# Dense gates, staging tiles and the last gathers of a PEER block: one-hots in one operation, token-innermost products, no separate end stage

## The chip, the cores and the metric

The kernel runs on one core of one Trainium2 chip. The metric is the device time of one execution in microseconds (us): a median of 3 runs of the kernel before is shown, and its profile comes from one further execution. A core has five engines, each with its own queue of instructions that it takes strictly in order: TensorE (PE in the rows, its weight loads PEld), VectorE (DVE), ScalarE (ACT), GpSimd (POOL) and SyncE (SP). Here SP issues the ordinary transfers and POOL the gathers of table rows.

## What is computed

The input is 1024 tokens of 1024 numbers. First a mixer: a normalisation, a projection to 1536 columns, a pooling half and a gated half, an output projection and a residual, giving `h`. Then the PEER layer, which most of this case is about:

```
q = (xb @ wq).reshape(T, 8, 2, 128)
s = einsum('thpd,phkd->thpk', q, keys)            # 8 heads, 2 lists of 128 keys
s_top, i_top = top_k(s, 16)                       # 16 of each list
best_s, best_pos = top_k(all 16*16 sums, 16)      # the best 16 pairs of each head
idx = 128 * key_of_list_0 + key_of_list_1         # one of 16384 experts
gate = softmax(best_s)
act = gelu(einsum('td,thkd->thk', xb, u_tab[idx]))
out = einsum('thk,thkd->td', gate * act, v_tab[idx])
```

So each token uses 128 experts (8 heads of 16), each a row of 4 KB in `peer_u` and one in `peer_v`. At the end the residual is added and the rows are normalised once more.

## The kernel before, in words

The 1024 tokens are 8 blocks of 128. The kernel treats them in two ways.

**Sparse blocks** 0, 1, 6 and 7 gather the rows they need. `sparse_u` (U0, U1, U6, U7) gathers 128 times 128 rows of `peer_u`; each gather of 512 KB is followed by one multiply-and-sum on DVE (`junk`, line 501). `sparse_v` (V0, V1, V6, V7) gathers rows of `peer_v` four gathers at a time, a quad; 8 matmuls into `po` (line 531) use up one quad, with a weight tile `wz` that ACT has written (line 520). There are two `wz` tiles, so that the write for quad j waits until the matmuls of quad j-2 are done. The gathered rows lie in a ring of 7 buffers (`rowt`), in the dense stage with 4 more (`rowv`), and after it in 16 (`rowe`).

**Dense blocks** 2 to 5 (512 tokens) multiply with all 16384 experts. For this `gates_dense` first builds the gate of every token and expert. For 4 tokens at a time it makes one-hot matrices of the two key lists (`oh`): on DVE one operation for all of list 0 (line 567), one for list 1 of two tokens (line 569) and one for each of the other two tokens with the gate multiplied in (line 581); ACT multiplies the gate into the first two (line 579). One matmul for each token (line 582) gives a 128 by 128 product in PSUM; two ACT operations (line 585) copy it into two half staging tiles `gs`, turned so that tokens are innermost. When 32 tokens are done, two transfers write the halves to the DRAM tensor `G` (line 589). This happens 128 times for 4 tokens, here called 128 groups, in four blocks of 32. Between the blocks DVE chooses the experts of the next block (`pick`).

Then `scale` multiplies the transposed activations `sd` by the row norms and splits them into two parts, `xdh` and `xdl`. `dense` runs over 128 chunks of 128 experts: load `raw_u` and `raw_v`, split each, 24 matmuls of 512 columns up (`mu<-xdh,...`), gelu, times the gates `gc` read back from `G` (line 645), split into `wh` and `wl`, and 24 matmuls down for each chunk, which are issued for three chunks together (`GROUP`), with the results added to `hD` on DVE (line 623).

What sets the order: the program is woven by generators (`weave`, `sparse`, `anchors`), and a scheduler orders the instructions of each engine from it. The plan `LATE` holds 704 gathers. While the dense chunks are written, 672 of them are called for; the last 32 (`AFTER`) are in a stage of their own behind the dense one, with new row buffers `rowe` in a pool that reuses the space of the dense stage.

```
        while done * NK < (c + 1) * (steps - AFTER):
    ...
    with tc.tile_pool(name="gae", bufs=EROWS, side="right", ...) as gae:
```

Of the kernel before, what the change touches and what calls it, by code (L numbers as in the profile page):

```python
# [47 lines left out]
GS = 3  # L48
# [5 lines left out]
ROWS, VROWS, EROWS = 7, 4, 16  # L54
# [12 lines left out]
def hybrid_block(ctx: ExitStack, tc: tile.TileContext, t: dict, out: bass.AP):  # L67
# [235 lines left out]
    def residual(fc, fr, chunks, most):  # L303
# [6 lines left out]
        for q in range(4):  # L310
            cols = slice(q * WC, (q + 1) * WC)
            for ch, p in zip(chunks, project(fr, "w_out", q * WC, [ch.a for ch in chunks], True)):
                nc.vector.tensor_add(ch.h[:, :, cols], ch.h[:, :, cols], p)

                def quarter(ch=ch, q=q, cols=cols):
                    hg = tmp(fr, 2 * WC).rearrange("p (k e) -> p k e", e=WC)
                    nc.vector.tensor_mul(hg, ch.h[:, :, cols], g2row[:, None, cols].to_broadcast([P, NB, WC]))
                    if not d0 <= ch.t0 // P < d0 + DBLK:
                        nc.sync.dma_start(gS[ch.t0:ch.t0 + N, cols].rearrange("(k p) e -> p k e", p=P), hg)
# [85 lines left out]
    def pick_heads(tk, top, tix, n, keys, gate_kh):  # L405
# [46 lines left out]
        for i in range(2):  # L452
            eq = tk.tile([P, TK, TK, PH], BF16, name="eq", tag="eq", bufs=1)[:, :, :, :n]
# [59 lines left out]
    def sparse_v(b):  # L513
# [4 lines left out]
        for j in range(32):  # L518
            z = wz[j % 2]
# [34 lines left out]
    def gates_dense(gp, b):  # L554
# [4 lines left out]
        for part in range(P // GT):  # L559
            kb = (b - d0) * (P // GT) + part  # L560
            gs = [gp.tile([P, NK // 2, GT], F32, name="gs", bufs=GS) for _ in range(2)]
            for t0 in range(0, GT, TB):

                oh = gp.tile([P, 2 * TB, NK], F32, name="oh", bufs=OH)
                tok = part * GT + t0
                half = TB // 2
                nc.vector.tensor_tensor(oh[:, 0:TB, :], iota_k[:, None, :].to_broadcast([P, TB, NK]),
                                        iT[:, 0, tok:tok + TB, None].to_broadcast([P, TB, NK]), op=ALU.is_equal)
                nc.vector.tensor_tensor(oh[:, TB:TB + half, :], iota_k[:, None, :].to_broadcast([P, half, NK]),
                                        iT[:, 1, tok:tok + half, None].to_broadcast([P, half, NK]), op=ALU.is_equal)  # L570
# [16 lines left out]
            for i, g in enumerate(gs):  # L587
                n = NK // GI // 2
                nc.sync.dma_start(G[i * n:(i + 1) * n, kb].rearrange("a i b t -> i a (b t)"),
                                  g.rearrange("i (a b) t -> i a (b t)", b=GI))  # L590

    def scale(tk, xdh, xdl):

        both = tk.tile([P, 2, ND], F32, name="both", tag="eq", bufs=1)
        r2B, x = both[:, 0, :], both[:, 1, :]
# [8 lines left out]
    def dense(de, xdh, xdl):
# [3 lines left out]
        with tc.tile_pool(name="da", bufs=2, side="right", reuse_waits="tile") as da:  # L608
# [17 lines left out]
            for c in range(NK):  # L626
# [240 lines left out]
```

## Time and profile before

| | us |
|---|---|
| median of 3 runs | 2702.26 (2700.18 to 2703.74) |
| the profiled execution, its own time | 2707.89 |
| its span in the trace | 2705.8 |
| PE busy | 2438.1, 90% of the span |
| DVE busy | 1896.4, 70% |
| POOL busy | 1198.3, 44% |
| ACT busy | 774.3, 29% |

The span is the time between the first and the last instruction of the trace. A busy share is an average over stages with different limits: in the mixer and the dense stage PE is the busy one, in the gates DVE, PE and the transfers share the work. Line numbers are those of the kernel before; in the changed kernel they are some lines lower.

### The profile page before, as it was taken

The numbers are of one execution on the slowest core, as the hardware profiler recorded it, in microseconds if no ns is written. First come the engines' busy times: TensorE is split into PE (matmuls) and PEld (weight loads), VectorE is DVE, ScalarE is ACT, GpSimd is POOL, SyncE is SP. The second block draws the span as 40 slices with busy tenths as digits, with TensorE's granted clock in tenths as the row PEclk, the third lists the DMA queues.
The fourth block names the chain that finished last, engine by engine and source line by source line (L and its number), as shares of the span: only waits on it lengthen the run. The fifth ranks groups of instructions, "written<-read, shape, count | busy, mean of one in ns | idle before, by whom it ended". The sixth has DMA issues, their size and how long they took to land.

```text
span 2705.8 us, 34765 instructions
## 1 busy us (share of the span) xinstructions
PE 2438.1 (90%) x11968; PEld 1862.7 (69%) x11968; DVE 1896.4 (70%) x4643; ACT 774.3 (29%) x1424; POOL 1198.3 (44%) x1098
## 2 busy tenths in 40 slices
PE   7997899888866467999999999999999999999993
PEld 6886788767645144777777777777777777766770
DVE  2389979987797977986776767666676766433451
ACT  3220011245635252222222222322222222222220
POOL 0034753143443544655555555465455555344004
PEclk9998999999978689999999999999999999999996
DMA  7677998599988799999999999899999999889317
GB/s 250 210 245 230 384 344 284 168 313 315 333 286 296 255 307 348 361 356 324 365 354 342 341 339 364 328 361 375 327 342 359 349 348 331 324 329 359 119 39 287
DMA packets 345392, 831.49 MB, mean 307 GB/s; under 512 B 25216, under 2 KB 158848, under 8 KB 345216
## 3 DMA queue, kind: packets, MB, share of 16 engines
q0 software_dynamic: 147456, 536.94, 54.0%
q1 hardware_dynamic: 197760, 292.33, 31.4%
q8 instruction: 95, 1.56, 0.2%
q14 instruction: 81, 0.66, 0.1%
HBM read 785.13 MB, written 44.04 MB: 306 GB/s over the span
## 4 chain that ended last, share of the span: by engine, by line
PE 67%; DVE 15%; DMA 9%; issue 5%; ACT 2%; POOL 1%; SPq 0%; POOLq 0%; ACTq 0%; DVEq 0%
PE mm L176 8%; PE mm L139 8%; PE mm L140 8%; PE mu L141 8%; PE mm L141 8%; PE mu L139 8%; PE mu L140 8%; PE po L531 8%; DVE junk L501 3%; DMA G<-gs 2%; DMA rowt<-peer_v,idxT 2%; DVE rest L372 1%; PE mm L582 1%; DMA w<-w_out 1%; PE mu L582 1%
## 5 line engine op out<-in xcount | busy, mean ns | idle before, releaser
L480 POOL DMA_INDIRECT rowt<-peer_v,idxT x432 | 500.5, 1159 | 709.0 <-PE po L531 501.6
L480 POOL DMA_INDIRECT rowv<-peer_u,idx x288 | 353.6, 1228 | 176.4 <-DVE junk L501 105.7
L480 POOL DMA_INDIRECT rowt<-peer_u,idx x224 | 261.4, 1167 | 346.5 <-DVE top L370 166.4
L139 PE MATMUL mm<-vh,wh 128*128 128x512 f32 x1024 | 400.8, 395 | 14.4 <-ACT wh L131 8.4
L141 PE MATMUL mu<-xdh,ul 128*128 128x512 f32 x1024 | 403.0, 394 | 6.6 <-DVE ul L132 6.6
L139 PE MATMUL mu<-xdh,uh 128*128 128x512 f32 x1024 | 401.2, 393 | 6.2 <-ACT xdh L131 3.7
L140 PE MATMUL mu<-xdl,uh 128*128 128x512 f32 x1024 | 401.8, 392 | 1.2 <-DVE xdl L132 0.7
L140 PE MATMUL mm<-vl,wh 128*128 128x512 f32 x1024 | 401.0, 392 | 0.1
L501 DVE SCALAR_TENSOR_TENSOR junk<-rowv,h 128x1024 bf16<-128x1024 f32 x288 | 352.0, 1222 | 44.2 <-DMA rowv<-peer_u,idx 41.2
L141 PE MATMUL mm<-vh,wl 128*128 128x512 f32 x1024 | 376.9, 392 | 0.0
L623 DVE TENSOR_TENSOR hD<-hD,mm 128x512 f32<-128x512 f32 x344 | 225.8, 682 | 184.4 <-PE mm L141 183.5
L501 DVE SCALAR_TENSOR_TENSOR junk<-rowt,h 128x1024 bf16<-128x1024 f32 x224 | 271.9, 1214 | 19.6 <-DMA rowt<-peer_u,idx 18.2
L531 PE MATMUL po<-rowt,wz 128*32 128x512 f32 x1728 | 237.8, 650 | 38.0 <-DMA rowt<-peer_v,idxT 38.0
L139 PEld LDWEIGHTS mm<-vh,wh 128*128 128x128 f32 x1024 | 193.0, 189 | 75.1 <-issue 14.2
L141 PEld LDWEIGHTS mu<-xdh,ul 128*128 128x128 f32 x1024 | 192.6, 188 | 65.8 <-DVE ul L132 9.4
L139 PEld LDWEIGHTS mu<-xdh,uh 128*128 128x128 f32 x1024 | 192.1, 188 | 58.7 <-issue 9.2
L140 PEld LDWEIGHTS mu<-xdl,uh 128*128 128x128 f32 x1024 | 192.8, 188 | 53.8 <-issue 9.2
L141 PEld LDWEIGHTS mm<-vh,wl 128*128 128x128 f32 x1024 | 192.6, 189 | 50.1 <-issue 9.2
L140 PEld LDWEIGHTS mm<-vl,wh 128*128 128x128 f32 x1024 | 193.2, 189 | 42.4 <-issue 2.5
L644 ACT ACTIVATE a<-mu 128x512 f32<-128x512 f32 x128 | 76.0, 594 | 491.2 <-PE mu L141 490.0
L132 DVE SCALAR_TENSOR_TENSOR ul<-raw_u,uh 128x1024 fp32r<-128x1024 f32 x128 | 156.2, 1220 | 78.3 <-ACT uh L131 78.3
L131 ACT ACTIVATE vh<-raw_v 128x1024 fp32r<-128x1024 f32 x128 | 131.0, 1052 | 235.8 <-PE mm L141 216.9
(167 smaller groups left out, 3374.3 us busy)
## 6 DMA issues: line engine op xcount, KB each, us to landing
raw_u<-uT SPq DMA_DIRECT2D x128, 512.0 KB, 6.9
raw_v<-peer_v SPq DMA_DIRECT2D x128, 512.0 KB, 7.2
G<-gs SPq DMA_DIRECT2D x32, 1024.0 KB, 14.8
w<-wq SPq DMA_DIRECT2D x48, 512.0 KB, 6.6
w<-w_in SPq DMA_DIRECT2D x36, 512.0 KB, 4.8
w<-w_out SPq DMA_DIRECT2D x24, 512.0 KB, 6.6
h<-x SPq DMA_DIRECT2D x16, 512.0 KB, 7.7
rowt<-peer_v,idxT POOLq DMA_INDIRECT x432
```

The costliest lines, as they stand in the source:

```text
L131: nc.scalar.activation(hi, src, AF.Copy)
L132: nc.vector.scalar_tensor_tensor(lo, src, 1.0, f32(hi), op0=ALU.mult, op1=ALU.subtract)
L139: nc.tensor.matmul(dst, lh, rh, start=first and c == 0, stop=False)
L140: nc.tensor.matmul(dst, lh, rl, start=False, stop=False)
L141: nc.tensor.matmul(dst, ll, rh, start=False, stop=last and c == n - 1)
L176: mm = nc.tensor.matmul(dst[:, i, :], lhs, rhs, start=c == 0, stop=c == NDC - 1)
L480: ins = nc.gpsimd.indirect_dma_start(out=rowt, out_offset=None, in_=t[table], in_offset=bass.IndirectOffsetOnAxis(ap=ids, axis=0))
L501: nc.vector.scalar_tensor_tensor(junk, r, 1.0, h, op0=ALU.mult, op1=ALU.mult, accum_out=act[:, j:j + 1])
L531: mm = nc.tensor.matmul(po[g * 32:(g + 1) * 32, q * HALF:(q + 1) * HALF], z[:, g, 31 - j:63 - j], r[:, q * HALF:(q + 1) * HALF], start=j = ...
L582: mm = nc.tensor.matmul(p[:, i, :], oh[:, i, :], c, start=True, stop=True)
L623: nc.vector.tensor_add(hq, hq, p)
L644: nc.scalar.activation(a, p, AF.Gelu_apprx_tanh)
```

## The change

Ten edits, as they stand in the diff:

- Gates: one DVE operation makes the one-hots of both lists for 4 tokens; ACT multiplies the gate into all four tokens; the products are written to PSUM with tokens innermost, as `p[:, :, i]`, so each matmul writes every fourth word; one ACT operation copies 4 tokens into a whole staging tile; one transfer of 2 MB writes 32 tokens to `G`. Two whole tiles take the place of three pairs' worth of halves (`GS = 3`, 2 at a time).
- Four `wz` tiles, not two.
- The activations of the middle tokens lie in a mixer tile, are also written to a DRAM tensor `sS`, and are read back by `scale` (4 loads). `scale` is called ahead of the remaining gates and no longer behind the last pick.
- `wh` and `wl` have 3 buffers, not 4.
- All 704 gathers of `LATE` are called for by chunk 125. The stage behind `dense`, its pool and `AFTER` are gone.

```
-    for i in range(2):
+    for i in range(4):
         z = const.tile([P, 4, 63], F32, name=f"wz{i}")
...
+                    if D0 <= ch.t0 < D0 + ND:
+                        nc.sync.dma_start(sS[2 * q:2 * q + 2, :, ch.t0 - D0:ch.t0 - D0 + N]
+                                          .rearrange("c p s -> p c s"), sq)
...
-            z = wz[j % 2]
+            z = wz[j % len(wz)]
...
-            gs = [gp.tile([P, NK // 2, GT], F32, name="gs", bufs=GS) for _ in range(2)]
+            gs = gp.tile([P, NK, GT], F32, name="gs", bufs=2)
...
-                nc.vector.tensor_tensor(oh[:, 0:TB, :], iota_k[:, None, :].to_broadcast([P, TB, NK]),
-                                        iT[:, 0, tok:tok + TB, None].to_broadcast([P, TB, NK]), op=ALU.is_equal)
-                nc.vector.tensor_tensor(oh[:, TB:TB + half, :], iota_k[:, None, :].to_broadcast([P, half, NK]),
-                                        iT[:, 1, tok:tok + half, None].to_broadcast([P, half, NK]), op=ALU.is_equal)
+                nc.vector.tensor_tensor(oh, iota_k[:, None, None, :].to_broadcast([P, 2, TB, NK]),
+                                        iT[:, 0:2, tok:tok + TB, None].to_broadcast([P, 2, TB, NK]), op=ALU.is_equal)
...
-                    p = ps.tile([P, TB, NK], F32, name="mm")
+                    p = ps.tile([P, NK, TB], F32, name="mm")
...
-                    if i < half:
-                        nc.scalar.activation(c, c, AF.Copy, scale=iT[:, 2, at])
-                    else:
-                        nc.vector.tensor_scalar(c, iota_k, iT[:, 1, at], iT[:, 2, at], op0=ALU.is_equal, op1=ALU.mult)
-                    mm = nc.tensor.matmul(p[:, i, :], oh[:, i, :], c, start=True, stop=True)
+                    c = oh[:, 1, i, :]
+                    nc.scalar.activation(c, c, AF.Copy, scale=iT[:, 2, tok + i:tok + i + 1])
+                    mm = nc.tensor.matmul(p[:, :, i], oh[:, 0, i, :], c, start=True, stop=True)
...
-                for g, cols in zip(gs, (slice(0, NK // 2), slice(NK // 2, NK))):
-                    nc.scalar.activation(g[:, :, t0:t0 + TB].rearrange("p k i -> p i k"), p[:, :, cols], AF.Copy)
+                nc.scalar.activation(gs[:, :, t0:t0 + TB], p, AF.Copy)
...
+        for c in range(0, NDC, 2):
+            x = de.tile([P, 2, ND], F32, name="raw_x", tag="raw", bufs=3)
+            nc.sync.dma_start(x, sS[c:c + 2].rearrange("c p s -> p c s"))
+            nc.vector.tensor_mul(x, x, r2B[:, None, :].to_broadcast([P, 2, ND]))
+            split(xdh[:, c:c + 2, :], xdl[:, c:c + 2, :], x)
...
-                wh = da.tile([P, ND], F32R, name="wh", bufs=GROUP + 1)
-                wl = da.tile([P, ND], F32R, name="wl", bufs=GROUP + 1)
+                wh = da.tile([P, ND], F32R, name="wh", bufs=GROUP)
+                wl = da.tile([P, ND], F32R, name="wl", bufs=GROUP)
...
+    scale(de, xdh, xdl)
     for _ in gates:
         pass
     for b in (6, 7):
         for _ in pick(tk, b):
             pass
         turn(b)
-    scale(tk, xdh, xdl)
...
-        while done * NK < (c + 1) * (steps - AFTER):
+        while done * (NK - GROUP) < min(c + 1, NK - GROUP) * steps:
             next(gathered, None)
             done += 1
-
-    with tc.tile_pool(name="gae", bufs=EROWS, side="right", reuse_waits="tile") as gae:
-        beside[:] = [(gae, "rowe", EROWS)]
-        homes["U"] = homes["V"] = beside[:]
-        for _ in gathered:
-            pass
```

The scheduler moves instructions on every engine. Three places matter below. The first is ACT's queue in the last block of gates, before (`oh` is the multiplication by the gate, `gs` the copy of products, `wz` the weight tile for a quad):

```order
L579 ACTIVATE oh<-oh,iT 128x128 x3
L520 ACTIVATE wz_87<-wT 128x4
L585 ACTIVATE gs<-mm 128x4x64
L585 ACTIVATE gs<-mu 128x4x64
L579 ACTIVATE oh<-oh,iT 128x128 x2
L585 ACTIVATE gs<-mm 128x4x64 x2
L585 ACTIVATE gs<-mu 128x4x64
```

and the same block with the change:

```order
L580 ACTIVATE gs<-mu 128x128x4
L577 ACTIVATE oh<-oh,iT 128x128 x8
L523 ACTIVATE wz_89<-wT 128x4
L580 ACTIVATE gs<-mm 128x128x4
L577 ACTIVATE oh<-oh,iT 128x128 x4
L580 ACTIVATE gs<-mu 128x128x4
```

The `wz` writes stand between gate work in both; with four tiles in turn each waits for a quad two further back, and a group has four multiplications and one copy in place of two and two.

The second is DVE's queue where the gates end and the dense stage begins, before (`both` and `xdl` are `scale`; `idxT` is the last turned list):

```order
L402 CAST idx<-key_6262 128x128
L468 CAST idxT<-mm 128x128
L601 TENSOR_TENSOR both<-sd,both 128x512
L132 SCALAR_TENSOR_TENSOR xdl<-both,xdh 128x512
L601 TENSOR_TENSOR both<-sd,both 128x512
L542 TENSOR_TENSOR h<-h,po 128x1024
L132 SCALAR_TENSOR_TENSOR xdl<-both,xdh 128x512
```

and with the change (`ul` and `vl` are splits of loaded chunks, `a` the product with the gates):

```order
L405 CAST idx<-key_6015 128x128
L471 CAST idxT<-mm 128x128
L504 SCALAR_TENSOR_TENSOR junk,act<-rowt,h 128x1024 x2
L131 SCALAR_TENSOR_TENSOR ul<-raw_u,uh 128x1024
L131 SCALAR_TENSOR_TENSOR vl<-raw_v,vh 128x1024 x2
L504 SCALAR_TENSOR_TENSOR junk,act<-rowt,h 128x1024 x2
L131 SCALAR_TENSOR_TENSOR vl<-raw_v,vh 128x1024
L639 TENSOR_TENSOR a<-a,gc 128x512 x2
```

The 8 pairs of `scale` are gone from here; as 4 pairs of double size they stand among the operations of the last pick. On PE three chunks of up-matmuls (72) stand ahead of the first down-matmul with the change, two (48) before; 29 quads of V0 stand ahead of the last gate matmuls with the change, all 32 before, and `wt` of U1 (the end of U1) moves from chunk 11.75 to 16.25.

The third is the end of POOL's queue, before:

```order
L480 DMA rowt<-peer_v,idxT 128x1024 x4
L480 DMA rowv<-peer_v,idxT 128x1024 x4
L480 DMA rowt<-peer_v,idxT 128x1024
L480 DMA rowe<-peer_v,idxT 128x1024 x32
L863 UNCONDITIONAL_BRANCH
```

and with the change:

```order
L483 DMA rowt<-peer_v,idxT 128x1024 x4
L483 DMA rowv<-peer_v,idxT 128x1024 x4
L483 DMA rowt<-peer_v,idxT 128x1024
L850 UNCONDITIONAL_BRANCH
L850 ISA
```

No gather uses `rowe` any more; on PE the last 8 quads, which stood behind the last dense matmul, now stand in pairs up to chunk 123.9. V7's 16 pairs stand between chunks 106.2 and 123.9 (1.18 chunks apart), before 12 pairs between 103.3 and 116.7 (1.22 apart).

## Rows read from the trace of the kernel before

**Rows 1.** The page's busy times: us, share of the span, instructions.

```profile
PE 2438.1 (90%) x11968; PEld 1862.7 (69%) x11968; DVE 1896.4 (70%) x4643; ACT 774.3 (29%) x1424; POOL 1198.3 (44%) x1098
```

**Rows 2.** The span cut at the ends of stages: from and to, length, busy us (and instructions) of each engine, granted share of TensorE's clock, busy share of the transfer engines, GB/s.

```profile
559.20:655.00 95.80, 82.03 (x506) 63.59 (x503) 67.37 (x181) 57.31 (x147) 36.43 (x35) 0.95 0.95 325
655.00:745.00 90.00, 77.67 (x468) 61.34 (x468) 74.78 (x257) 54.28 (x139) 36.32 (x32) 0.91 0.93 315
745.00:787.00 42.00, 20.66 (x105) 12.32 (x105) 38.15 (x166) 9.73 (x24) 17.36 (x18) 0.68 0.83 290
787.00:860.00 73.00, 59.47 (x363) 46.77 (x361) 58.44 (x195) 44.48 (x113) 31.58 (x28) 0.88 0.81 269
860.00:925.00 65.00, 21.23 (x99) 8.24 (x99) 59.97 (x291) 11.95 (x31) 28.45 (x25) 0.60 0.83 295
925.00:1013.60 88.60, 58.31 (x354) 40.31 (x358) 70.24 (x170) 47.18 (x126) 46.02 (x36) 0.81 0.87 293
1013.60:1048.00 34.40, 24.79 (x89) 13.60 (x81) 27.19 (x50) 12.63 (x20) 19.21 (x15) 0.95 1.02 366
1048.00:1200.00 152.00, 134.40 (x567) 105.82 (x568) 137.31 (x210) 38.01 (x50) 86.67 (x66) 0.97 0.96 351
1200.00:2300.00 1100.00, 1098.88 (x5261) 822.66 (x5260) 767.34 (x1106) 297.93 (x421) 601.44 (x503) 1.00 0.94 347
2300.00:2510.00 210.00, 210.00 (x1103) 148.25 (x1105) 87.14 (x119) 53.29 (x86) 89.06 (x87) 1.00 0.88 329
2510.00:2635.80 125.80, 125.70 (x564) 102.36 (x559) 62.26 (x93) 36.81 (x50) 0.00 (x0) 1.00 0.25 80
2635.80:2705.80 70.00, 23.40 (x129) 5.59 (x128) 12.84 (x51) 3.56 (x10) 29.96 (x32) 0.71 0.71 278
```

**Rows 3.** The end in order of time: start, duration, engine, line, operation, in brackets the idle time before and what ended it.

```profile
2495.57 0.94 POOL L480 DMA_INDIRECT rowt<-peer_v,idxT  x1 [0.31 <-PE mu L141]
2646.23 0.94 POOL L480 DMA_INDIRECT rowe<-peer_v,idxT  x1 [149.72 <-DMA out<-hD]
...
2635.43 0.39 PE L141 MATMUL mm<-vh,wl 128*128 128x512 f32 x1
...
2643.08 1.28 DVE L551 SCALAR_TENSOR_TENSOR hD<-hD,r,fgrow 128x1024 f32<-128x1024 f32 x1
...
2701.03 1.28 DVE L551 SCALAR_TENSOR_TENSOR h<-h,r,fgrow 128x1024 f32<-128x1024 f32 x1
```

**Rows 4.** PE in the middle of the dense stage, same columns: a quad and matmuls around it.

```profile
1816.23 1.94 PE L531 MATMUL po<-rowt,wz 128*32 128x512 f32 x16
1818.11 0.74 PE L141 MATMUL mm<-vh,wl 128*128 128x512 f32 x2
1818.69 0.40 PE L140 MATMUL mu<-xdl,uh 128*128 128x512 f32 x1
1818.92 0.40 PE L141 MATMUL mu<-xdh,ul 128*128 128x512 f32 x1
```

**Rows 5.** Gate work. First DVE at the first group in order of time, then groups of instructions over the whole span: line, engine, operation, out<-in, count, busy us, mean ns of one, idle time before.

```profile
559.19 0.69 DVE L567 TENSOR_TENSOR oh<-iota_k,iT 128x512 f32<-128x512 f32 x1
...
560.65 0.68 DVE L567 TENSOR_TENSOR oh<-iota_k,iT 128x512 f32<-128x512 f32 x1
...
L501 DVE SCALAR_TENSOR_TENSOR junk<-rowv,h 128x1024 bf16<-128x1024 f32 x288 | 352.0, 1222 | 44.2 <-DMA rowv<-peer_u,idx 41.2
...
L579 ACT ACTIVATE oh<-oh,iT 128x128 f32<-128x128 f32 x256 | 85.3, 387 | 36.0 <-DVE oh L569 35.5
...
L585 ACT ACTIVATE gs<-mm 128x256 f32<-128x256 f32 x128 | 71.8, 633 | 66.4 <-PE mm L582 33.4 <-DMA G<-gs 32.4
...
L644 ACT ACTIVATE a<-mu 128x512 f32<-128x512 f32 x128 | 76.0, 594 | 491.2 <-PE mu L141 490.0 <-DVE wl L132 1.2
...
L220 ACT ACTIVATE vn<-mm,r1s 128x256 f32<-128x256 f32 x16 | 6.7, 470 | 15.5 <-PE mm L176 15.5
...
L582 PE MATMUL mm<-oh 128*128 128x128 f32 x512 | 86.8, 316 | 36.4 <-ACT oh L579 36.4
```

**Rows 6.** Waits between 540 and 1030 us: engine, line waited for, us in total, times, longest.

```profile
ACT wz L520 <- PE po L531: 61.9, 20, 18.4
...
PE mm L582 <- ACT oh L579: 36.4, 24, 5.4
...
ACT gs L585 <- DMA G<-gs: 32.4, 9, 8.2
DVE oh L567 <- PE mm L582: 32.2, 14, 7.3
```

**Rows 7.** Two quads of V0 on PE, in order of time; four more stand between them.

```profile
865.49 3.67 PE L531 MATMUL po<-rowt,wz 128*32 128x512 f32 x16 [4.07 <-DMA rowt<-peer_v,idxT]
...
937.69 3.52 PE L531 MATMUL po<-rowt,wz 128*32 128x512 f32 x16 [2.91 <-DMA rowt<-peer_v,idxT]
```

**Rows 8.** Where the gates end: the last copies of products, the load of gates in the chain that ended last, and the first down-matmul.

```profile
1012.57 1.06 ACT L585 ACTIVATE gs<-mu 128x256 f32<-128x256 f32 x2 [1.02 <-PE mu L582]
...
1028.64 17.84 DMA gc<-G
...
1047.98 0.50 PE L139 MATMUL mm<-vh,wh 128*128 128x512 f32 x1 [0.98 <-ACT wh L131]
```

More of the change, by code (lines that the diff above doesn't have):

```diff
@@ L47 @@
 OH = 3
-GS = 3
 BEHIND = (3, 2)
 TURN = 6
-ROWS, VROWS, EROWS = 7, 4, 16
+ROWS, VROWS = 7, 4
 QUAD = 4
@@ L108, in hybrid_block @@
     gS = dram.tile([S, D], F32, name="gS")
+    sS = dram.tile([NDC, P, ND], F32, name="sS")
     G = dram.tile([NK // GI, ND // GT, P, GI, GT], F32, name="G")
@@ L317, in quarter @@
                     nc.vector.tensor_mul(hg, ch.h[:, :, cols], g2row[:, None, cols].to_broadcast([P, NB, WC]))
-                    if not d0 <= ch.t0 // P < d0 + DBLK:
+                    if not D0 <= ch.t0 < D0 + ND:
                         nc.sync.dma_start(gS[ch.t0:ch.t0 + N, cols].rearrange("(k p) e -> p k e", p=P), hg)
@@ L452, in pick_heads @@
         for i in range(2):
-            eq = tk.tile([P, TK, TK, PH], BF16, name="eq", tag="eq", bufs=1)[:, :, :, :n]
+            eq = tk.tile([P, TK, TK, PH], BF16, name="eq", bufs=1)[:, :, :, :n]
             nc.vector.tensor_tensor(eq, iota_a[:, :, None, :n].to_broadcast([P, TK, TK, n]),
@@ L560, in gates_dense @@
             kb = (b - d0) * (P // GT) + part
-            gs = [gp.tile([P, NK // 2, GT], F32, name="gs", bufs=GS) for _ in range(2)]
+            gs = gp.tile([P, NK, GT], F32, name="gs", bufs=2)
             for t0 in range(0, GT, TB):
-                oh = gp.tile([P, 2 * TB, NK], F32, name="oh", bufs=OH)
+                oh = gp.tile([P, 2, TB, NK], F32, name="oh", bufs=OH)
                 tok = part * GT + t0
-                half = TB // 2
-                nc.vector.tensor_tensor(oh[:, 0:TB, :], iota_k[:, None, :].to_broadcast([P, TB, NK]),
-                                        iT[:, 0, tok:tok + TB, None].to_broadcast([P, TB, NK]), op=ALU.is_equal)
-                nc.vector.tensor_tensor(oh[:, TB:TB + half, :], iota_k[:, None, :].to_broadcast([P, half, NK]),
-                                        iT[:, 1, tok:tok + half, None].to_broadcast([P, half, NK]), op=ALU.is_equal)
+                nc.vector.tensor_tensor(oh, iota_k[:, None, None, :].to_broadcast([P, 2, TB, NK]),
+                                        iT[:, 0:2, tok:tok + TB, None].to_broadcast([P, 2, TB, NK]), op=ALU.is_equal)
@@ L586, in gates_dense @@
                 yield
[L587 to L595, printed above, removed]
+            nc.sync.dma_start(G[:, kb].rearrange("a i b t -> i a (b t)"),
+                              gs.rearrange("i (a b) t -> i a (b t)", b=GI))
@@ L596, in scale @@
+    def scale(de, xdh, xdl):
+        r2B = de.tile([P, ND], F32, name="r2B", tag="a", bufs=2)
         p = ps.tile([P, HALF], F32, name="mm")[:, :ND]
@@ L599, in scale @@
         nc.scalar.activation(r2B, p, AF.Copy)
-        for c in range(NDC):
-            nc.vector.tensor_mul(x, sd[:, c, :], r2B)
-            split(xdh[:, c, :], xdl[:, c, :], x)
+        for c in range(0, NDC, 2):
[3 more added lines that the diff above has]
+            split(xdh[:, c:c + 2, :], xdl[:, c:c + 2, :], x)
     def dense(de, xdh, xdl):
@@ L748, in hybrid_block @@
     first = group(FIRST, ma[1:])
-    middle = group(MIDDLE, [sd[:, :, i * N:(i + 1) * N] for i in range(len(MIDDLE))])
     last = group(LAST, ma[1:])
@@ L753, in hybrid_block @@
     fc = opened(fcs, name="fc", bufs=1, side="right")
+    middle = group(MIDDLE, [fc.tile([P, NDC, N], F32, name=f"s{i}") for i in range(len(MIDDLE))])
     later.append(lambda: stats(0, NB))
```

9 lines of the change are left out of this document (3 added, 6 removed).

## The prediction

> **What bounds the kernel now.** I read the busy times first. PE is busy for 90% of the span [rows 1], so time can be won only where PE is idle or does work of another kind. Then I read the stretches. From 1200 to 2510 us PE is never idle (1098.9 of 1100 and 210.0 of 210 us) at full granted clock, so the dense stage is bound by its matmuls. What is added to PE there is paid in full; what DVE, ACT, POOL or the transfers (busy share 0.94) get there costs nothing as long as that holds [rows 2]. Two places have slack. One is the end: after the last dense matmul 70.0 us pass with PE busy for 23.4 of them [rows 2]. The other is the gates, the six stretches from 559.2 to 1013.6 us, 454.4 us long. Their PE times sum to 319.4 and their DVE times to 369.0 us; the transfers are busy for 0.81 to 0.95 of them, and no engine is full throughout [rows 2]. There I read the waits. ACT stands for 61.9 us at a `wz` write until a quad's matmuls have ended, and for 32.4 us at a copy into `gs` until a transfer to `G` has landed; behind it PE waits 36.4 us for scaled one-hots, and behind PE DVE waits 32.2 us for a one-hot buffer [rows 6]. So ACT's queue, which is far from full, holds up the two engines that are nearly full.
>
> **End stage.** POOL issues its last gather of the dense stage at 2495.57 us, then waits 149.72 us until `out<-hD` has read the space that `rowe` reuses, and starts the last 32 gathers at 2646.23 [rows 3]. Without that stage the dense end remains: the last matmul starts at 2635.43, the last `hD` operation ends at 2644.36, 8.6 us after the stretch's end at 2635.8. Then the output must be stored, for which I take what passes after the last operation now (2702.31 to the span's end at 2705.8, 3.5 us). So 12.1 of 70.0 us stay: **-57.9 us** [rows 2, 3].
>
> The 8 quads move to PE in the dense stage. A quad occupies PE there from 1816.23 to 1818.11, 1.88 us [rows 4]; with a little for the change of weights, 1.9 each: **+15.2 us**, on the path. Their gathers need room. From 2510 to 2635.8 POOL does nothing and the transfers are at 0.25 [rows 2], while 32 gathers of 512 KB are 16.8 MB, 48 us at the 347 GB/s of the long dense stretch. The order spaces V7's pairs as far apart as before (1.18 chunks against 1.22), and PE had no idle time at that spacing [rows 2], so I expect no wait there.
>
> **Gates, DVE.** A group's one-hots step by 1.46 us (559.19 to 560.65). One operation of 1024 columns is bounded by `junk`, also two inputs and 1024 columns, 1.22 us; consecutive ones overlap by about 0.08, as the steps show, so 1.14 [rows 5]. That saves 0.32 us for each of 128 groups, 10 us for each block of 32, 41 us in all.
>
> **Gates, ACT.** A group has two scalings (0.387) and two copies (0.633) now, 2.04 us; then four scalings and one copy. The copy of 512 contiguous words costs 0.594. The copies of 256 that write single words 128 bytes apart cost 0.633 where contiguous ones cost 0.470, so 0.64 ns more for each word [rows 5]. The new copy writes runs of four words. I bound it by 0.594 and 0.594 + 0.33 = 0.92 and take 0.65, nearest to the contiguous row: 2.20 us for a group, 20 us more in all. ACT is busy for 225 of 454 us [rows 2]; this is hidden.
>
> **Gates, waits.** With four `wz` tiles a write waits for the quad four back, two quads or some 29 us longer ago [rows 7], so nearly all of the 61.9 us go. With two whole staging tiles a copy waits for the transfer of two tiles back, not of half a tile: the 32.4 us go too. The 36.4 and 32.2 us behind them shrink [rows 6]. What is late next: in the first two stretches PE itself (82.0 of 95.8, 77.7 of 90.0) and the transfers (0.95, 0.93), so I take half of PE's idle time, 7 and 6 us. In the picks (745 to 787 and 860 to 925) DVE is full already; nothing is won, and `scale` comes into the second with 4 pairs of 1024 columns, 8 x 1.14 = 9 us, half of which I expect to find idle places: +5. From 787 to 860 DVE falls from 58 to 48 and PE has 59, so 62 of 73 us: -11. From 925 on DVE falls from 70 to 60, PE has 2 or 3 quads less than its 58, and 4.5 quads at 14.4 us each (865.49 to 937.69 is 5 steps) need 65: 66 of 88.6 us, -22 [rows 2, 7]. Sum **-41 us**, with ends at -10 (the gathers set the pace everywhere) and -65 (all of DVE's saving and half of what is left of its 85 idle us).
>
> **Token-innermost products.** Each of 1024 matmul instructions now writes every fourth word of PSUM. No row has such a write on PE. The nearest is ACT's copy above, 0.64 ns for each word set apart, which would be 82 ns for 128 columns and 84 us in all [rows 5]; the other end is nothing. [...]
>
> **Scale.** Moved ahead, it leaves the place where the gates end. There it hid behind the gates' way through DRAM anyway: the last copies start at 1012.57, `gc<-G` is loaded from 1028.64 for 17.84 us, and the first down-matmul starts at 1047.98 [rows 8]. That wait stays, so nothing is won by the move itself. In its shade PE can do a third chunk of up-matmuls (24 at 0.23, **-5.4 us**) [rows 4] and two of the three V0 quads that have come behind the gates; the third is paid, **+1.9 us**. U1 ends 4.5 chunks later; up to 1200 us, with U1 running, PE lost 17.6 of 152 us [rows 2], and for 54 us more of it I take **+4 us** (0 to 6). The 8 stores to `sS` (256 KB) and 4 loads add 4 MB, 12 us of transfers at 347 GB/s, beside matmuls; I put 0, ends -3 and +3.
>
> **`wh` and `wl`, 3 buffers.** The first `wh` of three chunks must now wait for the last down-matmul of the three before, as `vh` already does. At worst its 0.63 us comes ahead of `vh` each time, 42 times, 27 us; the order leaves PE 4.7 us of up-matmuls or more there nearly everywhere, so I take 0.
>
> **Sum.** -57.9 + 15.2 - 41 - 5.4 + 1.9 + 4 = -83.2 us. The profiled execution took 2707.89 (span 2705.8 and 2.1 around it), 5.6 above the median; the terms are differences, so I take them from the median: 2702.3 - 83.2 = **2619 us**, with 2598 to 2640 as its own range.
>
> **Rivals.**
> *The gathers pace the gates.* V0 uses the 7 row buffers almost one quad at a time, and PE waits for rows at both quads shown [rows 7]. If 21 quads keep the 15.7 us they have on average, the stage shrinks by 10 and not 41: 2650. Against it: with ACT free the quads come as soon as rows land.
> *Strided products, mildly slow.* 84 us on PE bring its work to 319 - 8 + 84, and with some 40 us of idle time the stage is 435: -19, time 2641. [...]
> *Strided products, very slow: slower than before.* The products occupy PE for about 170 us (twice 86.8). From 1.9 times that on, 146 us more, the stage is 497 us and eats the other gains (42.2 us). At three times it would be 691 us, the time 2897. For it: nothing hides PE there. Against it: PE would have to be held by writes alone.
> *The split waits.* 27 us in the dense stage: 2646.
> *The end stage does not vanish.* If the last quads wait for rows, up to 43 us come back: 2662. Against it is POOL's idle time from 2497 on.
>
> **How the numbers follow.** Forecast 0.66, gathers 0.11, mildly slow products 0.09, split 0.05, end 0.03, very slow products 0.06. A difference under 0.2% (5.4 us) can't be told from none: only a product price just near 1.9 times gives that, 0.02, of the last case, which leaves slower 0.05; all else is faster, 0.93. From 2590 to 2652 the range holds the forecast and most of the cases up to 2650.
>
> **What would show it.** Right: the last quads at full PE before the last down-matmul and some 12 us after it; ACT without `wz` waits in the gates; products at the same mean duration; the last copy of products near 970 us. Wrong: matmuls of the products lengthened; quads still 15 us apart or more with PE waiting for rows; PE idle between groups of three chunks.

## The result and the profile of the changed kernel

The changed kernel takes 2639.98 us (median of 4 runs, 2637.79 to 2640.96), the kernel before 2701.22 in the same runs: a ratio of 0.9772 (95% interval 0.9755 to 0.9789), 61.2 us less. The forecast was 2619 us, 83 us less; its range of 2590 to 2652 holds the time, its own range of 2598 to 2640 only with its upper end. The profiled executions, 2707.89 and 2640.66 us, are 67.2 us apart. The busy times of the changed kernel, to be read against [rows 1]:

```profile
PE 2421.6 (92%) x11968; PEld 1855.0 (70%) x11968; DVE 1855.1 (70%) x4251; ACT 788.4 (30%) x1548; POOL 1209.1 (46%) x1100
```

Its stretches follow, with the columns of [rows 2]. The cuts are the events of the changed kernel: first and second block of gates together, the pick for the third, the third block, the pick for the fourth, the fourth block up to the last copy of products, the seam up to the first down-matmul, then the dense stage and the end:

```profile
560.20:724.00 163.80, 147.36 (x923) 117.96 (x927) 115.29 (x224) 119.39 (x343) 76.21 (x57) 0.96 0.98 329
724.00:758.20 34.20, 16.98 (x99) 10.56 (x91) 33.89 (x163) 6.09 (x15) 14.10 (x13) 0.80 0.95 335
758.20:839.00 80.80, 68.81 (x421) 53.47 (x422) 61.74 (x142) 58.08 (x170) 48.43 (x36) 0.92 0.90 290
839.00:907.40 68.40, 16.56 (x75) 4.34 (x73) 59.03 (x261) 9.53 (x19) 25.26 (x22) 0.63 0.83 288
907.40:988.60 81.20, 59.65 (x362) 44.30 (x366) 65.67 (x90) 56.10 (x164) 46.08 (x34) 0.85 0.89 300
988.60:1019.30 30.70, 15.63 (x85) 10.49 (x77) 8.36 (x11) 7.20 (x9) 12.09 (x11) 0.80 0.97 328
1019.30:1200.00 180.70, 172.55 (x745) 137.40 (x749) 160.72 (x253) 48.05 (x66) 96.64 (x77) 0.98 0.96 354
1200.00:2300.00 1100.00, 1093.27 (x5224) 813.48 (x5217) 766.15 (x1104) 291.45 (x416) 595.97 (x507) 1.00 0.94 347
2510.00:2626.10 116.10, 115.75 (x582) 83.54 (x580) 53.37 (x91) 29.10 (x44) 27.57 (x29) 1.00 0.56 204
2626.10:2638.40 12.30, 0.00 (x0) 0.00 (x0) 8.45 (x37) 1.15 (x2) 0.00 (x0) 0.60 0.43 171
```

The gates of the kernel before, cut again at the same five events:

```profile
559.20:741.40 182.20, 156.10 (x950) 121.61 (x948) 138.56 (x422) 110.51 (x284) 69.76 (x64) 0.93 0.94 319
741.40:774.80 33.40, 15.24 (x88) 9.75 (x87) 33.15 (x159) 5.52 (x11) 13.11 (x13) 0.78 0.87 308
774.80:865.30 90.50, 69.72 (x408) 53.69 (x408) 72.34 (x242) 52.65 (x135) 39.97 (x36) 0.82 0.82 275
865.30:919.90 54.60, 17.92 (x83) 5.43 (x83) 49.78 (x253) 6.19 (x15) 23.50 (x21) 0.59 0.81 286
919.90:1013.60 93.70, 60.38 (x362) 42.09 (x366) 75.12 (x185) 50.07 (x134) 49.82 (x40) 0.79 0.87 293
```

From the two executions, with the forecast beside them:

| piece | before | after | difference | forecast |
|---|---|---|---|---|
| start to the first one-hot | 559.2 | 560.2 | +1.0 | 0 |
| gates: blocks 1 and 2 | 182.2 | 163.8 | -18.4 | |
| pick for block 3 | 33.4 | 34.2 | +0.8 | |
| block 3 | 90.5 | 80.8 | -9.7 | |
| pick for block 4 | 54.6 | 68.4 | +13.8 | |
| block 4 | 93.7 | 81.2 | -12.5 | |
| gates together | 454.4 | 428.4 | **-26.0** | **-41** |
| last copy to first down-matmul | 34.4 | 30.7 | -3.7 | 0 |
| first to last down-matmul | 1587.8 | 1606.8 | +19.0 | +15.7 |
| end | 70.0 | 12.3 | **-57.7** | **-57.9** |
| span | 2705.8 | 2638.4 | -67.4 | -83.2 |

The gates hold nearly all of the miss inside the profile, 15.0 of 15.8 us; what the other pieces missed cancels but for 0.8 us. The rest of the 21 us is the reference: the sum was taken off the median, and the profiled execution before was some 6 us above it.

What a group of four tokens costs now, by line, with the columns of [rows 5]: the one-hots, the scaling, the copy, the two kinds of products (L569, L577, L580 and L578 answer to L567, L579, L585 and L582):

```profile
L569 DVE TENSOR_TENSOR oh<-iota_k,iT 128x1024 f32<-128x1024 f32 x128 | 152.6, 1218 | 14.8 <-PE mm L578 11.2 <-PE mu L578 3.2
L577 ACT ACTIVATE oh<-oh,iT 128x128 f32<-128x128 f32 x512 | 159.9, 392 | 39.0 <-DVE oh L569 38.6
L580 ACT ACTIVATE gs<-mm 128x512 f32<-128x512 f32 x64 | 37.7, 589 | 16.0 <-PE mm L578 14.8
L578 PE MATMUL mm<-oh 128*128 128x128 f32 x512 | 84.1, 305 | 14.8 <-ACT oh L577 14.3
L578 PE MATMUL mu<-oh 128*128 128x128 f32 x512 | 81.3, 304 | 18.0 <-ACT oh L577 17.7
```

The one-hot of 1024 columns costs what `junk` costs, 1.22 us, as bounded by it. The products, each writing every fourth word, take 305 ns, not more than the 316 of [rows 5]. The copy of 512 words takes 589 ns where two of 633 stood. And the waits from 540 to 1030 us, as in [rows 6]:

```profile
ACT wz L523 <- PE po L534: 57.9, 13, 16.5
...
PE po L534 <- DMA rowt<-peer_v,idxT: 47.3, 13, 16.3
ACT oh L577 <- DVE oh L569: 38.6, 24, 7.6
...
PE mu L578 <- ACT oh L577: 17.7, 21, 2.2
PE mm L578 <- ACT oh L577: 14.3, 16, 4.2
...
DVE oh L569 <- PE mm L578: 11.2, 12, 3.7
```

ACT's wait for a transfer to `G` is gone, and the waits of PE for `mm` products and of DVE that stand in [rows 6] are less than half. But the wait at `wz`, which four tiles were to remove, is still 57.9 us, from 61.9.

Part of the shorter gates is work that moved: in the kernel before 28 quads of V0 and 56 row operations of U1 (`junk`) lie in the stage, with the change 26 and 54.

At the end PE works without a gap up to the last down-matmul, and the last operation follows 8 us later; these answer to [rows 3]:

```profile
2625.69 0.39 PE L140 MATMUL mm<-vh,wl 128*128 128x512 f32 x1
...
2633.35 1.28 DVE L554 SCALAR_TENSOR_TENSOR hD<-hD,r,fgrow 128x1024 f32<-128x1024 f32 x1
```

In the seam (from the last copy of products to the first down-matmul) three chunks of up-matmuls are done (72 matmuls from 982.89 to 1001.94, the first of them before the last copy), then one quad; from 1004.2 PE idles until 1019.27. The third chunk is no gain of the change: in the trace of the kernel before 72 up-matmuls stand ahead of the first down-matmul as well, not the 48 that the description of its order gives. PE's work on `mu` alone there (from and to, length, busy us and count, granted clock, transfers):

```profile
1013.60:1047.90 34.30, 23.02 (x72) 0.95 1.02 366
```

In the chain that ended last, in order of time, the last thing late there is a load of `raw_v`, issued while the last 2 MB of `G` were being written, not `gc` as in [rows 8]:

```profile
993.56 17.34 DMA raw_v<-peer_v
1010.90 1.06 ACT vh L130
...
1019.27 0.79 PE mm L138
```

### The profile page after: what moved, and what is told of

It reads as the page before. It is cut to its first block, busy times and chain, and to the rows that moved or that the text cites. A ratio compares the mean times of both kernels' runs of the same rounds, so it can differ in the third digit from the quotient of the medians.

```text
span 2638.4 us, 34312 instructions
## 1 busy us (share of the span) xinstructions
PE 2421.6 (92%) x11968; PEld 1855.0 (70%) x11968; DVE 1855.1 (70%) x4251; ACT 788.4 (30%) x1548; POOL 1209.1 (46%) x1100
## 4 chain that ended last, share of the span: by engine, by line
PE 67%; DVE 13%; DMA 11%; issue 5%; ACT 2%; POOL 1%; SPq 0%; DVEq 0%; POOLq 0%; ACTq 0%
PE mm L138 8%; PE mm L175 8%; PE mm L139 8%; PE po L534 8%; PE mu L140 8%; PE mm L140 8%; PE mu L138 8%; PE mu L139 8%; DMA rowt<-peer_u,idx 3%; DVE junk L504 3%; DMA rowt<-peer_v,idxT 2%; DMA rowv<-peer_u,idx 2%; PE mm L578 1%; PE mu L578 1%; DVE rest L375 1%
## 5 line engine op out<-in xcount | busy, mean ns | idle before, releaser
L483 POOL DMA_INDIRECT rowt<-peer_v,idxT x448 | 528.3, 1179 | 698.8 <-PE po L534 469.6
L140 PE MATMUL mm<-vh,wl 128*128 128x512 f32 x1024 | 371.0, 391 | 0.0
L534 PE MATMUL po<-rowt,wz 128*32 128x512 f32 x1792 | 243.2, 629 | 55.4 <-DMA rowt<-peer_v,idxT 47.3
L639 DVE TENSOR_TENSOR a<-a,gc 128x512 f32<-128x512 f32 x128 | 88.4, 691 | 152.9 <-ACT a L638 152.3
```

Source lines behind the costliest of these rows:

```text
L140: nc.tensor.matmul(dst, ll, rh, start=False, stop=last and c == n - 1)
L483: ins = nc.gpsimd.indirect_dma_start(out=rowt, out_offset=None, in_=t[table], in_offset=bass.IndirectOffsetOnAxis(ap=ids, axis=0))
L534: mm = nc.tensor.matmul(po[g * 32:(g + 1) * 32, q * HALF:(q + 1) * HALF], z[:, g, 31 - j:63 - j], r[:, q * HALF:(q + 1) * HALF], start=j = ...
L639: nc.vector.tensor_mul(a.rearrange("i (k t) -> i k t", t=GT), a.rearrange("i (k t) -> i k t", t=GT), gc[:, :, c % GI, :])
```

## Experiments

Each kernel was timed against the kernel before on the same chip. A ratio's interval is some 0.3% to 0.7% wide, so two variants of the changed kernel are told apart from about 10 us on; finer readings come from the stages of one profile each. For those, the gates of kernels with the gate code and plan of the changed one were 428.4, 429.3, 425.5 and 436.5 us (the last two with two weight tiles), and of the two with those of the kernel before 454.4 and 460.5: up to 7 us of scatter either way, with means 430 and 457. A stage of one profile that lies nearer to a mean than that is not told apart from it.

**The changed kernel once more**, beside some of the runs below.

> The changed kernel once more, on the chip of the next three, as their measure: 2640 us within 6, gates 428 us from the first one-hot to the last copy.

2651.1 us, ratio 0.9802 (0.9778 to 0.9826), gates 429.3 us. The time missed the expectation, the stage held it.

**1. The end stage alone.**

```
-        while done * NK < (c + 1) * (steps - AFTER):
+        while done * (NK - GROUP) < min(c + 1, NK - GROUP) * steps:
...
-    with tc.tile_pool(name="gae", bufs=EROWS, ...) as gae:
...
```

> Kernel before with one edit: all 704 gathers called for by chunk 125 and no end stage. Theory: the end falls from 70.0 to 12.3 us (-57.7), and the 8 quads cost 8 x 1.96 = 15.7 us of PE in the dense stage, so 2701.2 - 42 = 2659 us, with no wait for rows at the last quads. Rival (rows come late when 16 pairs are squeezed in): PE waits for rows in the last chunks, up to 43 us, 2665 to 2702 us.

2671.7 against 2709.1 us, ratio 0.9859 (0.9826 to 0.9892), 38 us less (29 to 47). The expected 42 lies inside the interval. Its last chunks and its end (columns of [rows 2]):

```profile
2500.00:2654.50 154.50, 154.40 (x751) 114.84 (x749) 71.99 (x114) 40.88 (x61) 29.19 (x30) 1.00 0.54 195
2654.50:2666.60 12.10, 0.02 (x1) 0.00 (x0) 8.44 (x37) 1.15 (x2) 0.00 (x0) 0.62 0.43 173
```

PE waits for no rows; the end is 12.1 us. This edit alone makes some 38 of the 61 us.

**2. Two weight tiles instead of four.**

```
-    for i in range(4):
+    for i in range(2):
         z = const.tile([P, 4, 63], F32, name=f"wz{i}")
```

> Changed kernel with two weight tiles in place of four. Theory: in the changed kernel ACT still waits 57.9 us at wz writes, so the tiles were not what freed the gates; with two the wait is some 60 to 100 us and the time 2640 to 2648 us. Rival (the forecast's view: the waits at wz held ACT, PE and DVE in the gates): 30 us or so come back, PE waits for scaled one-hots 60 us and more instead of 32, 2660 to 2670 us.

2640.1 us, ratio 0.9755 (0.9728 to 0.9782); gates 425.5. The wait at the write is 65.9 us, between the 57.9 and 66.6 of the changed kernel's two profiles, and neither the gates nor the time moves. The forecast's reading of that wait falls: what stood behind it in ACT's queue did not set the time.

```profile
ACT wz L523 <- PE po L534: 65.9, 15, 16.5
```

**3. Products contiguous, the copy turned.** The order of instructions on PE, DVE, ACT and POOL is unchanged, row for row.

```
-    p = ps.tile([P, NK, TB], F32, name="mm")
+    p = ps.tile([P, TB, NK], F32, name="mm")
...
-    mm = nc.tensor.matmul(p[:, :, i], oh[:, 0, i, :], c, start=True, stop=True)
+    mm = nc.tensor.matmul(p[:, i, :], oh[:, 0, i, :], c, start=True, stop=True)
...
-    nc.scalar.activation(gs[:, :, t0:t0 + TB], p, AF.Copy)
+    nc.scalar.activation(gs[:, :, t0:t0 + TB].rearrange("p k i -> p i k"), p, AF.Copy)
```

> Changed kernel with the products written contiguously, one token after the other, and the ACT copy turning them; the order of instructions on PE and DVE is the same. Theory (writing every fourth word costs PE nothing): the product matmuls keep their mean of 305 ns within 10 ns and their sum of 165 us; the copy goes from 589 to about 920 ns, 42 us more ACT work in the gates, most of it in ACT's idle time; total 2636 to 2655 us. Rival (the strided writes hold PE): the mean falls below 290 ns and the total to 2630 us or less.

2662.9 us, ratio 0.9830 (0.9801 to 0.9859), against 0.9755 for experiment 2 on the same chip: 23 us slower, more than either theory allowed. By line:

```profile
L578 PE MATMUL mm<-oh 128*128 128x128 f32 x512 | 88.0, 316 | 19.3 <-ACT oh L577 18.5 <-issue 0.6
L578 PE MATMUL mu<-oh 128*128 128x128 f32 x512 | 84.8, 313 | 34.3 <-ACT oh L577 31.1 <-issue 2.5 <-ACT gs L580 0.6
...
L580 ACT ACTIVATE gs<-mm 128x512 f32<-128x512 f32 x64 | 68.2, 1066 | 13.7 <-PE mm L578 12.6 <-remote 0.6
```

The contiguous products are not faster (316 and 313 ns against 305 and 304; from the start of one to the next 112 ns in the median in the kernel before, which writes them contiguously, and 112 in the changed one), so the strided ones cost PE nothing. That is measured for these FP32 matmuls of 128 columns. The copy costs 1066 ns instead of 589, 61 us in all, and that is not hidden: the gates take 445.8 us. ACT is busy for 294 of them, far from full, yet PE waits 31.1 + 18.5 us for scaled one-hots, not 17.7 + 14.3 (24.3 + 13.0 in the changed kernel's second profile), and DVE 23.5 + 11.5 for PE, not 11.2 + 3.2 (13.2 + 5.7):

```profile
PE mu L578 <- ACT oh L577: 31.1, 19, 5.8
...
PE mm L578 <- ACT oh L577: 18.5, 16, 4.2
...
DVE oh L569 <- PE mm L578: 23.5, 18, 4.4
...
DVE oh L569 <- PE mu L578: 11.5, 13, 1.8
```

**4. One-hots as before.**

```
-    nc.vector.tensor_tensor(oh, iota_k[:, None, None, :]..., iT[:, 0:2, tok:tok + TB, None]..., op=ALU.is_equal)
+    nc.vector.tensor_tensor(oh[:, 0], ..., iT[:, 0, tok:tok + TB, None]..., op=ALU.is_equal)
+    nc.vector.tensor_tensor(oh[:, 1, 0:half], ..., iT[:, 1, tok:tok + half, None]..., op=ALU.is_equal)
...
+    if i < half:
         nc.scalar.activation(c, c, AF.Copy, scale=...)
+    else:
+        nc.vector.tensor_scalar(c, iota_k, iT[:, 1, at], iT[:, 2, at], op0=ALU.is_equal, op1=ALU.mult)
```

> Changed kernel with the one-hots made as before (three kinds of DVE operation, the gate multiplied in on DVE for two of four tokens); products and the copy stay as changed. DVE gets some 41 us more in the gates, ACT 512 - 256 scalings less. Theory (DVE is the other half of what paces the gates): the gates go from 428 to 440 to 455 us, 2650 to 2667 us. Rival (the shorter ACT copies alone give the gain, as the run with contiguous products suggests): the gates stay at 428 or fall, 2630 to 2642 us.

2655.6 us, ratio 0.9815 (0.9787 to 0.9842), against 0.9802 for the changed kernel beside it: not told apart. In the gates:

```profile
568.20:1003.50 435.30, 310.91 (x1890) 226.43 (x1894) 374.60 (x1255) 182.70 (x452) 187.77 (x166) 0.84 0.93 311
```

DVE is busy for 374.6 us, 39 more than in the changed kernel, ACT for 66 less, and the stage is 435.3 us, 5 over the mean of 430, which is no more than the scatter; it also holds 27.5 quads of V0, not 26.25. The theory's 440 us or more and the rival's 428 or less are both missed, and the run does not decide between them. The DVE operation on which the forecast rested its 41 us is worth little by itself, or as much as the 256 scalings that it puts on ACT; the run can't part these two.

**5. `scale` called behind the picks again.**

```
-    scale(de, xdh, xdl)
     for _ in gates:
...
         turn(b)
+    scale(de, xdh, xdl)
```

> Changed kernel with one edit undone: scale is called behind the last picks again (it still loads from sS). Theory: the second pick shrinks from 68.4 to about 56 us, because 4 pairs of DVE work (9.7 us) and the waits for raw_x (9.4 us) leave it; behind the gates scale hides in the 30.7 us that the gates need through DRAM; the first down-matmul comes some 12 us earlier, 2628 us. Rival (gathers pace the gates): the pick shrinks but the last block of gates stretches by as much, 2640 us. Second rival (scale is needed behind the gates too): the up-matmuls wait for xdh, a chunk less fits into the shade, 2640 to 2650 us.

2635.7 us, ratio 0.9737 (0.9710 to 0.9765), not told apart from experiment 2. The stage did as expected and the total did not. The last pick takes 46.2 us and the gates 413.7, but the up-matmuls must now wait for the fourth `raw_x` behind the last gates: last copy to first down-matmul is 43.9 us, not 30.7. From the first one-hot to the first down-matmul it is 457.6 us, with one chunk of up-matmuls in it and not three; the changed kernel has 459.1.

**6. `scale` cut in two**, loads where they are, arithmetic behind the eighth-last one-hot.

```
+    scaled = scale(de, xdh, xdl)
+    next(scaled)
     for _ in gates:
...
+    with tc.issue_after(ohs[-8]):
+        for _ in scaled:
+            pass
```

> Changed kernel with scale cut in two: its four loads stay where they are (the fourth into a tile of its own), its arithmetic on DVE and ACT comes behind the 8th-last one-hot instead of into the last pick. Theory: the last pick falls from 68 to about 56 us, the last block stretches by at most 5, and since the loads are done the up-matmuls start at the last copy as now: first down-matmul some 8 to 13 us earlier, 2627 to 2632 us. Rival (gathers pace the gates, the pick's time comes back in the last block): 2638 to 2642 us.

2642.4 us, ratio 0.9786 (0.9754 to 0.9818), against 0.9802: not told apart. Block 3, the pick and block 4, first here, then in the changed kernel beside it (here the pick is cut from the start of the last one-hot before it, in the tables above from its end, which makes it 1.2 us shorter):

```profile
764.50:846.40 81.90, 68.29 (x417) 52.41 (x418) 60.43 (x140) 56.87 (x168) 47.98 (x36) 0.92 0.89 279
846.40:892.40 46.00, 13.77 (x64) 4.07 (x63) 45.96 (x248) 4.55 (x14) 16.95 (x15) 0.70 0.86 307
892.40:990.80 98.40, 65.34 (x375) 45.16 (x376) 76.87 (x102) 62.08 (x172) 59.28 (x40) 0.83 0.89 297
```

```profile
762.40:850.10 87.70, 70.26 (x409) 54.17 (x410) 60.86 (x140) 56.38 (x164) 46.60 (x36) 0.85 0.87 281
850.10:910.20 60.10, 19.17 (x88) 6.33 (x86) 60.10 (x265) 11.79 (x24) 25.55 (x22) 0.59 0.88 306
910.20:990.30 80.10, 57.86 (x362) 42.66 (x366) 65.56 (x90) 55.88 (x164) 46.06 (x34) 0.88 0.91 304
```

The pick gives back 14 us, the last block takes 18 (with 6 quads of V0 in it, not 5.25). So the place of `scale` lengthens the pick, but undoing that gains nothing. The rival said so and put it down to the gathers, which experiments 8, 9 and 11 test.

**7. An eighth of the gates stored.**

```
-    nc.sync.dma_start(G[:, kb]..., gs...)
+    n = NK // GI // 8
+    nc.sync.dma_start(G[0:n, kb]..., gs[:, 0:NK // 8]...)
...
-    G[c // GI]
+    G[c // GI % (NK // GI // 8)]
```

> Changed kernel that stores only an eighth of each staging tile to G (28 MB less) and reads the same eighth for every chunk, so that most gates are left out. Theory (transfers pace the first two blocks, where their share is 0.99 and 0.96): these blocks fall from 85.5 and 78.3 us towards PE's 75 and 72, gates 410 to 418 us, and behind them the way through G gets shorter by 5 to 12 us: 2612 to 2628 us. Rival (transfers pace nothing in the gates): gates 425 to 430 us, 2628 to 2638 us, all of it behind the gates.

2648.1 us, ratio 0.9797 (0.9772 to 0.9821): no gain. The gates took 446.5 us at a transfer share of 0.78, the seam 11.5. Both theories missed: the scheduler, knowing the stores small, put 29 quads of V0 between the first and the last gate work, not 26, so that the stage holds other work. The sum, 458.0 us to the first down-matmul, is that of the changed kernel, with one quad more in it. Less transfer load did not speed up this part of the program, but the stage itself is not a clean comparison.

**8 and 9. Fewer gathers beside the gates**, in the kernel before and in the changed one.

```
-EARLY = ({"U0": 128}, {"V0": 128, "U1": 64})
-LATE = ({"U1": 64}, ...
+EARLY = ({"U0": 128}, {"V0": 128, "U1": 32})
+LATE = ({"U1": 96}, ...
```

> Kernel before with one number changed in its plan: 32 instead of 64 rows of U1 are called for beside V0, the other 32 in the dense stage; every operation of the gates stays as it was. By the order 145 rows are used between the first and the last gate work, not 166. Theory (gathers pace the gates, 2.7 us for each row issued in every run so far): gates 454 x 145/166 = 397 us, and 2645 to 2660 us in all, as the dense stage pays something for 32 more gathers. Rival (the waits at wz, gs and one-hots pace them, as the forecast had it): DVE has 21 row operations of 1.2 us less, gates 430 to 454 us, 2680 to 2710 us.

> Changed kernel with the same number changed (32 rows of U1 beside V0). By the order 145 rows in the gates, not 156, with all 32 quads of V0 among them. Theory (gathers pace): gates 428 x 145/156 = 398 us, 3 quads less behind them, 2605 to 2620 us. Rival (the change has freed the gates of everything but PE, DVE and ACT work): gates 415 to 428 us, 2630 to 2645 us.

Before: 2701.2 against 2712.3 us, ratio 0.9969 (0.9948 to 0.9990), gates 435.2 us. Changed: 2636.6 us, ratio 0.9714 (0.9685 to 0.9743), gates 431.1 us. A pace of 2.7 us for each gather would have given 397 and 398; the theory, formed after the runs above because their gates all took 2.5 to 2.8 us for each gather issued, falls in both. With 29 row operations of U1 on DVE in the gates in place of 56, the gates of the kernel before lose some 22 us, of which part comes back in the seam (45.9 us, where the two profiles with the old plan have 34.4 and 40.7); the changed kernel's (29 in place of 54) lose nothing, with 3 quads more inside. Its ratio is the lowest of all runs, but its interval meets that of the next run on the same chip, which has the plan of the changed kernel; the changed kernel itself was not timed on that chip, so whether the smaller plan is faster is not shown.

**10. Four buffers of `wh` and `wl`**, two `wz` tiles to make the room.

```
-                wh = da.tile([P, ND], F32R, name="wh", bufs=GROUP)
+                wh = da.tile([P, ND], F32R, name="wh", bufs=GROUP + 1)
```

> Changed kernel with two wz tiles and four buffers of wh and wl (the space of the two wz tiles makes room for them). Theory (the third buffer is what PE waits for in the long dense stretch): PE's idle time from 1200 to 2300 us falls from 6.7 us to about 1, and 2634 to 2638 us. Rival (these waits come from DVE and ACT being late with other work): it stays at 5 to 7 us, 2640 us.

2646.8 us, ratio 0.9743 (0.9708 to 0.9778); from 1200 to 2300 us PE is idle for 7.8 us (1100 - 1092.15), 6.7 and 9.4 in the two profiles with three. The rival's reading holds: the idle time does not come from the third buffer.

**11. Eight row buffers**, two `wz` tiles.

```
-ROWS, VROWS = 7, 4
+ROWS, VROWS = 8, 4
```

> Changed kernel with eight row buffers in place of seven (two wz tiles, as in an earlier run that cost nothing, make the room). By the order 27 quads of V0 lie in the gates, 26 in the changed kernel. In ten runs so far with the plan of U1 unchanged the gates took 15.4 to 17.1 us for each quad that the order puts there. Theory (the ring of row buffers paces the quads and these the gates: four rows and two of U1 go round through 7 buffers in 16.4 us): with 8 buffers a quad takes 14.4 us, the gates 27 x 14.4 = 388 us, 2600 to 2615 us in all. Rival (the quads only follow a pace that PE, DVE and ACT set in the gates): 425 to 445 us, 2636 to 2652 us.

2677.2 us, ratio 0.9888 (0.9864 to 0.9912): slower. In the gates the waits for rows did fall, PE's for quads from 47.3 to 30.2 us,

```profile
PE po L534 <- DMA rowt<-peer_v,idxT: 30.2, 9, 9.4
```

and yet the stage takes 426.0 us where 388 were expected. The ring of row buffers does not pace the gates; the quads follow. In the dense stage PE is idle for 28.9 us of the 1100 from 1200 on, mostly waiting for splits and products of ACT and DVE; why an eighth buffer does that is open.

## Why the prediction was right and where it failed

**End stage and quads: right.** 57.7 us gone, 57.9 forecast. A quad holds PE for 1.97 us (the start of the next matmul less that of the one before and one step of 0.227), so 8 take 15.7, 15.2 forecast (1.88 each from the rows; the 0.02 for the change of weights was an estimate), and no rows come late. Experiment 1 measures the two together: 38 us, 29 to 47, where 42 follow from the rows.

**Gates: the right sign, 26 us of 41, and the wrong reasons.** The step that failed is **Gates, waits**. It read ACT's 61.9 us at `wz` as time that held up PE and DVE; they are 57.9 and 66.6 us in the two profiles with four tiles and 65.9 with two, at the same time of the kernel (experiment 2). The 32.4 us at `gs` did go, but no run puts the half staging tiles back, so what that was worth is not known. In the sum two terms were mis-sized. The last block was to lose 22 us, by 4.5 quads at 14.4 us each; it lost 12.5 and 13.6 in the two profiles, and holds 5.25 quads at 15.4. The pick was to grow by 5 us for `scale`: it grew by 13.8 in this execution, with DVE idle for 9.4 us ahead of two operations on `raw_x`, and by 4.3 in the second profile (58.9 us, measured the same way), where block 3 lost 1.6 us and not 9.7. The first two blocks lost 18.4 and 16.0 us, 13 forecast. The four blocks together lost 40.6 us in the first profile, 46 forecast.

**Gates, DVE** was right in the operation, 1.22 us; its worth is not shown: with 39 us of it put back and 66 us of ACT's work taken off, the stage grew by about 5 (experiment 4). **Gates, ACT** counted the new copy among 20 us more of ACT's work that would be hidden. Of the edits in the gates that were undone it mattered most: with a copy 0.48 us longer for each group the stage grew by 16 and the time by 23 us (experiment 3). The two copies of the kernel before took 1.27 us for a group, so 0.48 of 0.68 us were put back. An engine that is busy for 249 of 428 us was in the path here: each group passes through it twice, between DVE and PE and then before the product's buffer comes free.

So of 27 us (means 457 and 430) experiment 3 takes 16 back and experiment 4 about 5. These are single profiles with up to 7 us of scatter, and effects need not add. The rest is staging, the two quads that moved out, scatter or what the scheduler made of it. What sets the remaining pace is open. From the first one-hot to the first down-matmul it took 489 and 501 us with the gates of the kernel before, and 459 and 460 in the changed kernel, which has one quad and 8 to 10 row operations of U1 less in it. Less transfer, an eighth row buffer, fewer gathers, two weight tiles and another place of `scale` left it at 452 to 458, the other copy made it 474. The other one-hots made it 470. Both are hardly apart from the 467 of experiment 10, whose gate code is unchanged; for the copy the time of the kernel tells them apart.

**Products: right.** The sum has no term for them, and there is no cost, now measured both ways (305 and 304 ns strided, 316 and 313 contiguous). Why writing every fourth word costs PE nothing, no run shows.

**Scale and seam.** The -5.4 us for a third chunk of up-matmuls had nothing to gain: the trace of the kernel before has three chunks there too. Two of the three late V0 quads fit in as forecast and one is paid. The seam is 3.7 us shorter, and its bound is another: `raw_v` behind the last stores; with an eighth stored it is 11.5 us (experiment 7), which agrees. From the first to the last down-matmul 19.0 us were added, 15.7 forecast, and that the two lie near each other is luck. The +4 us for a longer U1 came out with the other sign: up to 1200 us PE is idle for 8.2 of 180.7 us, where it was for 17.6 of 152.0. Nine more quads hold PE for 17.7 us, and from 1200 to 2300 PE has 5.6 us of new idle time, which four `wh` buffers do not remove. **The split, three buffers: right**, no cost that experiment 10 could take away.

**Signs and rivals.** Of the signs of being right, the last quads at full PE, the 12 us behind them and the products' mean came out; ACT kept its `wz` waits, and the last copy of products ended at 988.6 us, not near 970. One sign of being wrong came out: V0's quads are 16.3 us apart in the gates (26.25 in 428.4 us), with PE waiting 47.3 us for rows. In the kernel before they were 16.1 apart (28.3 in 454.4); the rival's 21 quads at 15.7 are not what the trace has. Yet *the gathers pace the gates* (2650) does not hold as a mechanism, since neither fewer gathers nor more buffers move the stage as such a pace would (experiments 8, 9 and 11). Nor does *strided products, mildly slow* (2641), whose time is the one measured: the products are not slower. A number that fits is no evidence for the mechanism that gave it. That holds for the forecast too: the time lies just at the upper end of the forecast's own range, and inside the wide one through room that was left for rivals which did not come.

## What to carry to other kernels

An end stage that waits for a buffer can be priced from its own rows; here such a price held within 0.2 us. A wait of a half-empty engine is worth something only if an instruction behind it is one that others wait for: see who gets idle behind it before counting it as gain. Where small groups of work pass through several engines, look at the operations that lie between the engines, whatever the busy share of the engine that does them: here 0.48 us for each of 128 groups cost 16 us. And count in the trace what already stands in a gap before pricing what will fit there.

## What the runs showed of the hardware

ACT's copy of 512 words from PSUM takes 589 ns when it writes runs of four words (the changed kernel) and 1066 when it writes single words 128 bytes apart (experiment 3), 0.93 ns more for each word; [rows 5] had suggested 0.64. Single words cost more here and in [rows 5]; why, no run shows.

In the changed kernel's profile PE did no work for 15.07 us up to 1019.27 us. Its granted clock was 0.50 in the 4.8 us from 1019.3, and 1.00 from 1024.5 to 1038. That is one gap; what set the clock is not shown. The matmuls of the first stretch were issued 0.43 us apart, not 0.23, some 2.4 us lost at the start of the dense stage (columns of [rows 2]):

```profile
1019.30:1024.10 4.80, 4.80 (x11) 3.77 (x12) 2.63 (x4) 1.75 (x3) 3.58 (x5) 0.50 1.04 401
1024.50:1038.00 13.50, 13.50 (x61) 11.17 (x60) 5.41 (x8) 1.71 (x2) 0.30 (x1) 1.00 0.94 346
```
